# Attention values projected with tokens on partitions in one block, and keys kept in natural order

## The chip, the cores and the metric

The kernel runs on one core of a Trainium2 chip. The metric is device time in microseconds (us), the median of repeated runs. Engines are TensorE (PE in the rows, with PEld for its weight loads), VectorE (DVE), ScalarE (ACT), GpSimd (POOL) and SyncE (SP), which issues most of the DMAs.

## What is computed

One decoder layer: two token mixers run side by side on a normalised input, stick-breaking attention with 8 heads of 64 and a gated delta rule with 4 heads of 128, on 1024 tokens of 1024 channels. Both results are gated, projected, merged and projected once more. Cut to the part that the change touches:

```python
h    = rms_norm(x, pre_w)
proj = h @ w_in                         # all projections of both mixers, gates, merge gates
# stick-breaking attention, for each block of 128 queries and all keys up to it
z = einsum('bhqd,bhkd->bhqk', qb, kb) * scale
causal = k_pos < q_pos
log_keep = where(causal, -softplus(z), 0)
suffix = cumsum(log_keep, axis=3, reverse=True) - log_keep   # sum over the later keys
a = where(causal, exp(log_sigmoid(z) + suffix), 0)
o = einsum('bhqk,bhkd->bhqd', a, vb)
```

So a key's weight is sigmoid(z) times the product of sigmoid(-z) over all keys that lie between it and the query: a running product from the latest key back to the first.

## The kernel before

Every matrix product of a projection is made in three parts, since each operand is kept as a rounded value and its rest (`hi`, `lo`): hi·hi, hi·lo, lo·hi. `dense` (L224 and on, its product at L231) computes one half of a projection, 128 channels x 512 tokens, as 8 x 3 = 24 products of 128x512. Its weight slice is loaded by `load_w` (a DMA of 512 KB on SP's queue into one of two `raw` buffers, a cast on ScalarE, a subtraction on VectorE). A dense result lies in one of three PSUM buffers of pool `psd`. All other PSUM tiles, the scores `z`, the transposes `aT` and the results `av`, take turns in the five buffers of pool `psg`: a tile takes the buffer of the fifth one before it, and has to wait until that one has been read.

The normalised input `h` (`h_hi`, `h_lo`) lies with channels on partitions, so it serves as moving operand with the weights as stationary one, and the result has channels on partitions. Per pair of heads `p` (four pairs) the attention takes four projections: `sb_k` (keys, written in reversed token order, so that the latest key comes first), `sb_v` (values, channels on partitions, also reversed), `sb_g` (the branch gate; between its two halves the 8 transposes of `svT` that give `svn`, values with tokens on partitions) and `sb_q`. `fill(n)` is n projections of the merge gates (`mg`), 16 in all, that nothing in the attention needs; they are used as filler.

In the attention, `sb_z(p, g, a)` takes queries 256 g to 256 g + 255 of head `a` of the pair, in two blocks `qb`: score products into `z` pieces of at most 512 keys, two sigmoids of each on ScalarE (`kp`, what is kept; `bt`, what is taken), one scan on VectorE that turns `kp` into the running product (L812), one product on GpSimd that multiplies it into `bt` (L813). The names of the tiles carry these numbers: `z_2_0_7_1` is pair 2, head 0, block 7, second piece. `sb_av(p, g)` transposes `bt` tile by tile (`aT`, from tile c = 7 downward), copies each out of PSUM (odd c on VectorE, even c on ScalarE, the last two with the causal mask on VectorE) and multiplies it with `svn` into `av`. It runs one g behind: the transposes of g stand after the scores of g + 1.

The order on TensorE is what the generators write. `weave` takes steps of two generators in turn so that both progress in proportion to two given costs: here the attention of pair p, and a side chain that holds the projections of pair p + 1 and one filler (four fillers beside the last pair). Ahead of that stand the delta rule's scan, woven with `sb_k(0)` and `sb_v(0)`, then `sb_g(0)`, `sb_q(0)`, the delta rule's output and its branch projections `yb(0..7)`, and behind it the attention's branch projections (`ya`) and the output projection.

## Time and profile before

| | |
|---|---|
| median of three runs | 948.19 us (947.26 to 949.79) |
| profiled execution, its time | 947.04 us |
| its span, first to last instruction | 945.2 us |
| TensorE busy | 926.2 us, 98% of the span |
| VectorE / ScalarE / GpSimd busy | 588.6 / 384.4 / 167.0 us |
| 64 scans on VectorE | 101.9 us |
| 64 products on GpSimd behind them | 104.1 us |
| 32 transposes of `svT` on TensorE | four groups of 8, from 409.6 to 671.3 us |

The four pairs of the attention take about 475 to 548, 548 to 631, 631 to 714 and 714 to 803 us of the span, the branch projections `yb` 428 to 475, the output projection the last 95 us. Busy time of TensorE counts instructions that overlap their neighbour once; the pitch, from one start to the next, is what one costs. Idle time on an engine that nobody waits for costs nothing.

### The profile page before, as it was taken

What the parts mean: (1) busy time and instruction counts of PE and PEld (TensorE: products, weight loads), DVE (VectorE), ACT (ScalarE), POOL (GpSimd) and SP (SyncE); (2) the same over time, 40 slices, a digit from 0 to 9 for tenths busy, and PEclk for the clock granted to TensorE, in tenths of its full rate; (3) what the DMA queues carried; (4) which work ended last, traced back from release to release, by engine and by line L of the source; (5) the groups of instructions that cost most, each with busy time, mean ns of one, the idle gap of its engine ahead of it and who ended that gap; (6) DMA issues with size and microseconds to landing.
All of it is one profiled execution on the core that took longest, in us unless ns stands there. A gap on an engine that the chain in (4) does not pass through costs nothing.

```text
span 945.2 us, 13426 instructions
## 1 busy us (share of the span) xinstructions
PE 926.2 (98%) x5194; PEld 761.9 (81%) x5194; DVE 588.6 (62%) x1058; ACT 384.4 (41%) x853; POOL 167.0 (18%) x113
## 2 busy tenths in 40 slices
PE   8999999999999999999999999999999999999997
PEld 7968888788787887888888778877887887778886
DVE  5669895366999933656466634873684573953244
ACT  6666441145555112543254423543462453422121
POOL 1021210001113000000133212431332350441000
PEclk9999999999999999999999999999999999999999
DMA  8014214300232341015620111020101213841352
GB/s 261 10 46 123 79 67 134 68 24 23 68 78 76 109 104 37 23 45 204 219 68 23 45 45 45 23 68 23 45 23 45 90 45 125 303 160 36 102 182 96
DMA packets 84194, 80.12 MB, mean 85 GB/s; under 512 B 16969, under 2 KB 70306, under 8 KB 84130
## 3 DMA queue, kind: packets, MB, share of 16 engines
q1 hardware_dynamic: 80272, 70.55, 24.0%
q10 hardware_dynamic: 3858, 8.72, 2.7%
q8 instruction: 41, 0.67, 0.3%
q14 instruction: 23, 0.19, 0.1%
HBM read 60.88 MB, written 18.37 MB: 84 GB/s over the span
## 4 chain that ended last, share of the span: by engine, by line
PE 84%; DVE 9%; ACT 2%; issue 2%; DMA 1%; POOL 1%; DVEq 0%; POOLq 0%; ACTq 0%
PE d_mg L231 17%; PE y L1001 9%; PE d_sv L231 5%; PE d_sk L231 5%; PE d_gg L231 5%; PE d_sgt L231 5%; PE d_yb L231 4%; PE d_sq L231 4%; PE d_v L231 4%; PE av L842 3%; PE aT L829 3%; PE d_k L221 3%; PE d_k L231 2%; PE z L806 2%; PE z L807 2%
## 5 line engine op out<-in xcount | busy, mean ns | idle before, releaser
L813 POOL TENSOR_TENSOR bt<-bt,kp 128x127 f32<-128x127 f32 (+3 forms) x64 | 104.1, 1635 | 380.5 <-ACT bt L810 192.9
L812 DVE TENSOR_TENSOR_SCAN kp<-kp,mscan 128x128 f32<-128x128 f32 (+3 forms) x64 | 101.9, 1605 | 25.9 <-ACT kp L809 25.6
L231 PE MATMUL d_mg<-h_hi,whi_mg 128*128 128x512 f32 x256 | 101.5, 396 | 1.0 <-ACT mg L686 1.0
L231 PE MATMUL d_mg<-h_lo,whi_mg 128*128 128x512 f32 x256 | 99.9, 390 | 0.0
L231 PE MATMUL d_mg<-h_hi,wlo_mg 128*128 128x512 f32 x256 | 99.8, 390 | 0.0
L809 ACT ACTIVATE kp<-z 128x384 f32<-128x384 f32 (+4 forms) x96 | 48.2, 502 | 44.8 <-PE z L807 41.2
L231 PEld LDWEIGHTS d_mg<-h_hi,whi_mg 128*128 128x128 f32 x256 | 48.1, 188 | 12.5 <-issue 1.7
L231 PEld LDWEIGHTS d_mg<-h_hi,wlo_mg 128*128 128x128 f32 x256 | 48.1, 188 | 10.2
L231 PEld LDWEIGHTS d_mg<-h_lo,whi_mg 128*128 128x128 f32 x256 | 48.1, 188 | 9.2
L1001 PE MATMUL y<-wohi,m_lo 128*128 128x512 f32 (+1 forms) x136 | 51.3, 377 | 0.0
L1001 PE MATMUL y<-wohi,m_hi 128*128 128x512 f32 (+1 forms) x136 | 51.3, 377 | 0.0
L1001 PE MATMUL y<-wolo,m_hi 128*128 128x512 f32 (+1 forms) x136 | 51.2, 377 | 0.0
L810 ACT ACTIVATE bt<-z 128x384 f32<-128x384 f32 (+4 forms) x96 | 48.7, 508 | 3.7 <-DMA mB_d<-mb 1.7
L379 POOL TENSOR_TENSOR acc_k<-acc_k,pre_k 128x1024 f32<-128x1024 f32 x4 | 9.6, 2388 | 166.0 <-ACT pre_k L378 166.0
L842 PE MATMUL av<-aT,svn 128*64 128x256 f32 (+1 forms) x320 | 36.8, 366 | 1.1 <-DVE aT L835 1.1
L829 PE MATMUL aT<-ident,bt 128*128 128x128 f32 x288 | 36.6, 273 | 1.1 <-DVE sgT L849 0.6
L829 PEld LDWEIGHTS aT<-ident,bt 128*128 128x128 f32 x288 | 32.9, 140 | 5.7 <-issue 2.5
L89 DVE TENSOR_TENSOR wlo_mg<-raw_mg,whi_mg 128x1024 fp32r<-128x1024 f32 x16 | 24.3, 1517 | 20.3 <-ACT whi_mg L88 20.3
L1005 ACT ACTIVATE yj<-y 128x512 f32<-128x512 f32 (+1 forms) x17 | 9.7, 573 | 62.9 <-PE y L1001 56.6
L964 POOL TENSOR_TENSOR sA<-sA,mBl 128x512 f32<-128x512 f32 x16 | 25.5, 1606 | 48.7 <-DMA mBl<-mB_d 26.5
L842 PEld LDWEIGHTS av<-aT,svn 128*64 128x64 f32 x320 | 20.7, 136 | 15.8 <-issue 4.9
L686 ACT ACTIVATE mg<-d_mg 128x512 f32<-128x512 f32 x32 | 19.2, 602 | 30.9 <-PE d_mg L231 30.4
(379 smaller groups left out, 2450.3 us busy)
## 6 DMA issues: line engine op xcount, KB each, us to landing
raw_mg<-in_w_in_dram SPq DMA_DIRECT2D x16, 512.0 KB, 4.2
mg_d<-mg ACTq DMA_DIRECT2D x16, 512.0 KB, 2.9
x<-in_x_dram SPq DMA_DIRECT2D x8, 512.0 KB, 6.2
mb<-mg_d SPq DMA_DIRECT2D x8, 512.0 KB, 5.9
mB_d<-mb SPq DMA_DIRECT2D x8, 512.0 KB, 2.6
rawo<-in_w_out_dram SPq DMA_DIRECT2D x8, 512.0 KB, 4.4
sA<-mg_d SPq DMA_DIRECT2D x8, 512.0 KB, 7.1
mBl<-mB_d SPq DMA_DIRECT2D x8, 512.0 KB, 7.5
```

Source lines behind the costliest of these rows:

```text
L89: nc.vector.tensor_sub(lo[:, :nk], raw[:, :nk], hi[:, :nk].bitcast(F32))
L221: nc.tensor.matmul(ps, lhsT=a[:, k], rhs=b[:, c0:c1], start=(k == 0 and i == 0), stop=(k == nk - 1 and i == 2))
L231: nc.tensor.matmul(ps, lhsT=a[:, k], rhs=b[:, hs], start=(k == 0 and i == 0), stop=(k == nk - 1 and i == 2))
L686: nc.scalar.activation(gt[:, hs], ps, AF.Sigmoid)
L809: nc.scalar.activation(kp[:, os_], ps[:, :pc], AF.Sigmoid, scale=-0.125)
L810: nc.scalar.activation(bt[:, os_], ps[:, :pc], AF.Sigmoid, scale=0.125)
L812: nc.vector.tensor_tensor_scan(kp[:, :n], kp[:, :n], mscan[:, :n], 1.0, op0=ALU.mult, op1=ALU.max)
L813: nc.gpsimd.tensor_tensor(bt[:, 1:n], bt[:, 1:n], kp[:, 0:n - 1], op=ALU.mult)
L829: nc.tensor.transpose(ps[:, (a * 2 + j) * P:(a * 2 + j + 1) * P], at[p, a, qb][:, off:off + P], ident)
L842: nc.tensor.matmul(av[a * 64:(a + 1) * 64, j0 * P:2 * P], lhsT=vn[:, c, a * 64:(a + 1) * 64], rhs=aT[:, a * 2 + j0:a * 2 + 2], start=(c == ...
L964: nc.gpsimd.tensor_tensor(ga[:, hs], ga[:, hs], mb[:, hs], op=ALU.add)
L1001: nc.tensor.matmul(ps, lhsT=a[:, k, ts_], rhs=b[:, c0:c1], start=(k == 0 and i == 0), stop=(k == NK - 1 and i == 2))
```

## The change

Values are projected once, ahead of the attention, with the other operand stationary: a tile of 128 tokens of `h` is stationary and the weights of all 512 value channels move, so the result has tokens on partitions and needs no transpose. `load_wv` loads the weights in four pieces of 512 KB, after `yb(1)` to `yb(4)`, and splits them; `sb_v` then makes 8 token tiles of 24 products, each copied out by ScalarE. Keys and values stay in natural order. The scan runs over a reversed view of `kp`, the product on GpSimd reads the next column where it read the one before, the causal mask is mirrored, and the transposes take their columns from the other end.

The side chains of the attention lose the value projections, and the fillers are dealt out anew: one beside the delta rule in place of `sb_v(0)`, one after `sb_g(0)` in place of `sb_q(0)`, which moves behind the value block; one beside each of pairs 0 and 1, none beside pair 2, three beside pair 3. One is left for after the attention, as before.

```diff
-                                fill=0.0, base=-P, channel_multiplier=1)
+                                fill=0.0, base=-1, channel_multiplier=-1)
...
-            rs = slice((1 - half) * HT, (2 - half) * HT)
+            hs = slice(half * HT, (half + 1) * HT)
...
-                nc.scalar.copy(K[a][s, rs][:, ::-1], ps[s])
-                nc.vector.tensor_sub(K[a][d, rs][:, ::-1], ps[s], K[a][s, rs][:, ::-1].bitcast(F32))
+                nc.scalar.copy(K[a][s, hs], ps[s])
+                nc.vector.tensor_sub(K[a][d, hs], ps[s], K[a][s, hs].bitcast(F32))
...
-    def sb_v(p):
-        vT = slot(f"svT_{p}")
-        w = load_w(win[:, 1024 + p * P:1024 + (p + 1) * P], NK, f"sv{p}")
-        for half in range(2):
-            rs = slice((1 - half) * HT, (2 - half) * HT)
-            ps = yield from dense(w, NK, hk, half, f"sv{p}")
-            nc.scalar.copy(vT[:, rs][:, ::-1], ps)
-        sbd[p].append(vT)
+    wv, sv = [], []
+
+    def load_wv(k2):
+        with tc.high_priority(offset=ahead[0]):
+            raw = wp.tile([P, 2, HT], F32, tag="raw", name=f"raw_sv{k2}")
+            nc.sync.dma_start(raw, win[k2 * 2 * P:(k2 + 1) * 2 * P, 1024:1536].rearrange("(k p) c -> p k c", p=P))
+            hi = slot(f"svhi_{k2}", F32R, shape=[P, 2, HT])
+            lo = slot(f"svlo_{k2}", F32R, shape=[P, 2, HT])
+            nc.scalar.copy(hi, raw)
+            nc.vector.tensor_sub(lo, raw, hi.bitcast(F32))
+        for k in range(2):
+            wv.append((hi[:, k], lo[:, k]))
+
+    def sb_v():
+        for t in range(NT):
+            ts_ = slice(t * P, (t + 1) * P)
+            if t % 2 == 0:
+                sv.append(slot(f"sv_{t}", shape=[P, 2, HT]))
+            ps = psd.tile([P, HT], F32, tag="d", name=f"d_sv_{t}")
+            for k in range(NK):
+                rh, rl = hk(k)
+                for i, (a, b) in enumerate(((rh, wv[k][0]), (rh, wv[k][1]), (rl, wv[k][0]))):
+                    nc.tensor.matmul(ps, lhsT=a[:, ts_], rhs=b, start=(k == 0 and i == 0),
+                                     stop=(k == NK - 1 and i == 2))
+                yield 0.64
+            nc.scalar.copy(sv[t // 2][:, t % 2], ps)
...
-            if half == 0:
-                vT = sbd[p].pop()
-                vn = slot(f"svn_{p}", shape=[P, NT, P])
-                for g in range(2):
-                    ps = gps(f"svp_{p}_{g}")
-                    for j in range(4):
-                        c = g * 4 + j
-                        nc.tensor.transpose(ps[:, j * P:(j + 1) * P], vT[:, c * P:(c + 1) * P], ident)
-                    nc.vector.tensor_copy(vn[:, g * 4:g * 4 + 4], ps.rearrange("p (c j) -> p c j", j=P))
-                sbd[p].append(vn)
...
-    stages = (sb_k, sb_v, sb_g, sb_q)
+    stages = (sb_k, sb_g, sb_q)
...
-                nc.vector.tensor_tensor_scan(kp[:, :n], kp[:, :n], mscan[:, :n], 1.0, op0=ALU.mult, op1=ALU.max)
-                nc.gpsimd.tensor_tensor(bt[:, 1:n], bt[:, 1:n], kp[:, 0:n - 1], op=ALU.mult)
+                kr = kp[:, :n][:, ::-1]
+                nc.vector.tensor_tensor_scan(kr, kr, mscan[:, :n], 1.0, op0=ALU.mult, op1=ALU.max)
+                nc.gpsimd.tensor_tensor(bt[:, 0:n - 1], bt[:, 0:n - 1], kp[:, 1:n], op=ALU.mult)
...
-                    off = c * P - (T - (qb + 1) * P)
+                    off = (NT - 1 - c) * P
...
-    weave(sc, 37, chain(sb_k(0), sb_v(0)), 20.5)
+    weave(sc, 37, chain(sb_k(0), fill(1)), 20.5)
     g_n(1)
-    drain(sb_g(0), sb_q(0))
+    drain(sb_g(0), fill(1))
     g_o(2)
     g_o(3)
-    drain(*[yb(m) for m in range(NK)])
+    for m in range(NK):
+        drain(yb(m))
+        if 1 <= m <= 4:
+            load_wv(m - 1)
+    drain(sb_v(), sb_q(0))
...
-        side = chain(*[f(p + 1) for f in stages], fill(1)) if p + 1 < NP else fill(4)
-        weave(until_none(att), 24.0, side, 52.0 if p + 1 < NP else 41.0)
+        side = chain(*[f(p + 1) for f in stages], fill(p < 2)) if p + 1 < NP else fill(3)
+        weave(until_none(att), 24.0, side, (40.0 if p < 2 else 30.0))
```

Three places show how this moves instructions. The numbers at the ends of the names are buffer numbers.

TensorE, pair 2, between the transposes of tile 5 and of tile 4 of g = 1, before. All 27 dense products that stand there belong to the query projection of pair 3; the last three are shown.

```order
L231 MATMUL d_sq3_1_6280<-h_hi_189,whi_sq3_6241 128x512
L231 MATMUL d_sq3_1_6280<-h_lo_190,whi_sq3_6241 128x512
L231 MATMUL d_sq3_1_6280<-h_hi_189,wlo_sq3_6242 128x512
L829 MATMUL aT_2_1_4_6284<-ident_111,bt_2_0_3_6009 128x128
L829 MATMUL aT_2_1_4_6284<-ident_111,bt_2_1_3_6074 128x128
L806 MATMUL z_2_0_6_0_6290<-KA_2_5161,QH_2_1_5664 128x448
```

The same place after, all of it:

```order
L837 MATMUL aT_2_1_5_6293<-ident_111,bt_2_1_3_6167 128x128
L231 MATMUL d_sgt3_1_6238<-h_hi_189,whi_sgt3_6136 128x512
L231 MATMUL d_sgt3_1_6238<-h_lo_190,whi_sgt3_6136 128x512
L231 MATMUL d_sgt3_1_6238<-h_hi_189,wlo_sgt3_6137 128x512
L231 MATMUL d_sgt3_1_6238<-h_hi_189,whi_sgt3_6136 128x512
L231 MATMUL d_sgt3_1_6238<-h_lo_190,whi_sgt3_6136 128x512
L231 MATMUL d_sgt3_1_6238<-h_hi_189,wlo_sgt3_6137 128x512
L231 MATMUL d_sq3_0_6313<-h_hi_189,whi_sq3_6309 128x512
L231 MATMUL d_sq3_0_6313<-h_lo_190,whi_sq3_6309 128x512
L231 MATMUL d_sq3_0_6313<-h_hi_189,wlo_sq3_6310 128x512
L837 MATMUL aT_2_1_4_6317<-ident_111,bt_2_0_3_6110 128x128
L837 MATMUL aT_2_1_4_6317<-ident_111,bt_2_1_3_6167 128x128
```

Of the 27 dense products 9 are left; in pair 3 they go from 18 to 9. Between the transposes of tile 6 and of tile 5 of g = 2, ahead of `av`, they go from 18 to 9 in pairs 2 and 3, and stay 18 in pairs 0 and 1.

VectorE, pair 2, g = 2 and the two longest scans of head 1 (`kp_2_1_6`, `kp_2_1_7`), before:

```order
L89 TENSOR_TENSOR wlo_mg3_6542<-raw_mg3_6539,whi_mg3_6541 128x1024
L740 TENSOR_TENSOR QL_3_1_6354<-d_sq3_1_6280,QH_3_1_6353 64x512
L741 TENSOR_TENSOR QL_3_1_6354<-d_sq3_1_6280,QH_3_1_6353 64x512
L812 SCALAR_TENSOR_TENSOR kp_2_1_6_6343<-kp_2_1_6_6343,mscan_127 128x896
L835 COPY aT_2_2_7_6417<-aT_2_2_7_6418 128x512
L812 SCALAR_TENSOR_TENSOR kp_2_1_7_6402<-kp_2_1_7_6402,mscan_127 128x1024
L835 COPY aT_2_2_5_6450<-aT_2_2_5_6451 128x512
```

And after:

```order
L740 TENSOR_TENSOR QL_3_0_6387<-d_sq3_0_6313,QH_3_0_6386 64x512
L741 TENSOR_TENSOR QL_3_0_6387<-d_sq3_0_6313,QH_3_0_6386 64x512
L820 SCALAR_TENSOR_TENSOR kp_2_1_6_6367<-kp_2_1_6_6367,mscan_127 128x896
L740 TENSOR_TENSOR QL_3_0_6387<-d_sq3_0_6313,QH_3_0_6386 64x512
L741 TENSOR_TENSOR QL_3_0_6387<-d_sq3_0_6313,QH_3_0_6386 64x512
L843 COPY aT_2_2_7_6425<-aT_2_2_7_6426 128x512
L820 SCALAR_TENSOR_TENSOR kp_2_1_7_6410<-kp_2_1_7_6410,mscan_127 128x1024
L843 COPY aT_2_2_5_6447<-aT_2_2_5_6448 128x512
```

The query projection of pair 3 now stands later against the attention, and two of its subtractions have come between the two scans.

ScalarE at the start of the attention, after (before, the first sigmoids stood among the branch weights' casts, `whi_wbg4` and `whi_wbg6`, long after the casts of Q):

```order
L739 CAST QH_0_0_4735<-d_sq0_0_4710 64x512
L88 CAST whi_sgt1_4973<-raw_sgt1_4971 128x1024
L738 CAST QH_0_1_4770<-d_sq0_1_4745 64x512
L739 CAST QH_0_1_4770<-d_sq0_1_4745 64x512
L816 ACTIVATE kp_0_0_0_4780<-z_0_0_0_0_4782 128x128
L817 ACTIVATE bt_0_0_0_4781<-z_0_0_0_0_4782 128x128
```

The first sigmoids now stand behind a weight cast and two casts of the query projection's second half.

## Rows read from the trace of the kernel before

**Rows 1.** The page: busy time and share; the chain that ended last, by engine

```profile
PE 926.2 (98%) x5194; PEld 761.9 (81%) x5194; DVE 588.6 (62%) x1058; ACT 384.4 (41%) x853; POOL 167.0 (18%) x113
PE 84%; DVE 9%; ACT 2%; issue 2%; DMA 1%; POOL 1%; DVEq 0%; POOLq 0%; ACTq 0%
```

**Rows 2.** Two stretches: length, busy PE, PEld, DVE, ACT, POOL, granted clock, DMA

```profile
631.00:714.00 83.00, 82.69 (x453) 66.56 (x451) 50.33 (x55) 37.64 (x78) 26.62 (x16) 1.00 0.14 39
714.00:797.00 83.00, 82.69 (x454) 66.33 (x454) 43.84 (x41) 34.21 (x71) 26.61 (x16) 1.00 0.20 64
```

**Rows 3.** The chain in order of time: start, length, engine, what

```profile
416.09 10.88 PE d_sq L231 x48
...
856.23 80.12 PE y L1001 x366
```

**Rows 4.** Timeline of PE, start and length; line 781 (min/median/max ns)

```profile
512.70 1.03 PE L780 MATMUL svp<-ident,svT 128*128 128x128 f32 x8
513.49 0.48 PE L231 MATMUL d_sgt<-h_hi,whi_sgt 128*128 128x512 f32 x1
...
L781 DVE COPY svn<-svp x8: 683/688/692, 410.2 to 672.4; 128x512 f32<-128x512 f32 x8
```

**Rows 5.** Lines 753 and 740 on DVE: min/median/max ns

```profile
L753 DVE TENSOR_TENSOR KA<-d_sk,KA x8: 683/685/685, 373.0 to 652.0; 64x512 fp32r<-64x512 f32 x8
L753 DVE TENSOR_TENSOR KB<-d_sk,KB x8: 692/694/694, 374.4 to 653.3; 64x512 fp32r<-64x512 f32 x8
...
L740 DVE TENSOR_TENSOR QL<-d_sq,QH x16: 674/690/696, 422.8 to 702.6; 64x512 fp32r<-64x512 f32 x16
```

**Rows 6.** Timelines of PE and of DVE, pair 3, g = 1

```profile
754.86 0.30 PE L806 MATMUL z<-KB,QH 128*128 128x320 f32 x1
...
762.78 0.40 PE L806 MATMUL z<-KA,QH 128*128 128x512 f32 x1
...
761.43 0.99 DVE L833 TENSOR_TENSOR aT<-aT,mdiag 128x512 f32<-128x512 f32 x2
```

**Rows 7.** Timelines of PE and of DVE, pair 3, g = 2

```profile
781.65 1.95 PE L842 MATMUL av<-aT,svn 128*64 128x256 f32 x16
...
781.33 0.66 DVE L835 COPY aT<-aT 128x512 f32<-128x512 f32 x1
```

**Rows 8.** Timelines of PE, DVE and POOL, pair 2, g = 2

```profile
710.05 2.14 PE L842 MATMUL av<-aT,svn 128*64 128x256 f32 x16
...
693.39 2.98 DVE L812 TENSOR_TENSOR_SCAN kp<-kp,mscan 128x1024 f32<-128x1024 f32 x1
...
706.66 3.81 DVE L812 TENSOR_TENSOR_SCAN kp<-kp,mscan 128x1024 f32<-128x1024 f32 x1
710.39 0.66 DVE L835 COPY aT<-aT 128x512 f32<-128x512 f32 x1
...
692.10 2.12 POOL L813 TENSOR_TENSOR bt<-bt,kp 128x895 f32<-128x895 f32 x1 [4.38 <-DVE kp L812]
...
706.19 2.12 POOL L813 TENSOR_TENSOR bt<-bt,kp 128x895 f32<-128x895 f32 x1 [7.25 <-ACT aT L837]
```

**Rows 9.** Timelines of PE and ACT; line 738 (min/median/max ns)

```profile
432.38 0.22 PE L806 MATMUL z<-KA,QH 128*128 128x128 f32 x1
...
548.00 1.05 ACT L88 CAST whi_sv<-raw_sv 128x1024 fp32r<-128x1024 f32 x1 [4.66 <-PE d_mg L231]
...
549.44 0.27 ACT L809 ACTIVATE kp<-z 128x128 f32<-128x128 f32 x1
...
L738 ACT CAST QH<-d_sq x16: 579/582/585, 421.6 to 701.3; 64x512 fp32r<-64x512 f32 x16
```

**Rows 10.** Waits of PE: total us, times, longest

```profile
PE av L842 <- DVE aT L835: 1.1, 1, 1.1
```

**Rows 11.** The page's scans (busy, mean ns); DMA issues, us to landing

```profile
L812 DVE TENSOR_TENSOR_SCAN kp<-kp,mscan 128x128 f32<-128x128 f32 (+3 forms) x64 | 101.9, 1605 | 25.9 <-ACT kp L809 25.6
...
raw_sv<-in_w_in_dram SPq DMA_DIRECT2D x4, 512.0 KB, 4.2
```

More of the change, by code (lines that the diff above doesn't have):

```diff
@@ L772, in sb_g @@
             nc.vector.tensor_tensor(gT[:, hs], gT[:, hs], ps, op=ALU.mult)
-            if half == 0:
-                vT = sbd[p].pop()
-                vn = slot(f"svn_{p}", shape=[P, NT, P])
-                for g in range(2):
-                    ps = gps(f"svp_{p}_{g}")
-                    for j in range(4):
-                        c = g * 4 + j
-                        nc.tensor.transpose(ps[:, j * P:(j + 1) * P], vT[:, c * P:(c + 1) * P], ident)
-                    nc.vector.tensor_copy(vn[:, g * 4:g * 4 + 4], ps.rearrange("p (c j) -> p c j", j=P))
-                sbd[p].append(vn)
         sbd[p].append(gT)
         osb.append(gT)
-    stages = (sb_k, sb_v, sb_g, sb_q)
+    stages = (sb_k, sb_g, sb_q)
     at = {}
     def sb_z(p, g, a):
-        K, vn, gT, Q = sbd[p]
+        K, gT, Q = sbd[p]
         QH, QL = Q[g // 2]
@@ L796, in sb_z @@
                 n = (qb + 1) * P
-                c0 = T - n
                 qs = slice((qb % 4) * P, (qb % 4 + 1) * P)
@@ L803, in sb_z @@
                 for i in range(npc):
-                    cs = slice(c0 + i * pc, c0 + (i + 1) * pc)
+                    cs = slice(i * pc, (i + 1) * pc)
                     ps = gps(f"z_{p}_{a}_{qb}_{i}")
@@ L811, in sb_z @@
                     yield 2 * pc / 2400 + 0.06 * (i == 0)
-                nc.vector.tensor_tensor_scan(kp[:, :n], kp[:, :n], mscan[:, :n], 1.0, op0=ALU.mult, op1=ALU.max)
-                nc.gpsimd.tensor_tensor(bt[:, 1:n], bt[:, 1:n], kp[:, 0:n - 1], op=ALU.mult)
+                kr = kp[:, :n][:, ::-1]
+                nc.vector.tensor_tensor_scan(kr, kr, mscan[:, :n], 1.0, op0=ALU.mult, op1=ALU.max)
+                nc.gpsimd.tensor_tensor(bt[:, 0:n - 1], bt[:, 0:n - 1], kp[:, 1:n], op=ALU.mult)
                 at[p, a, qb] = bt
     def sb_av(p, g):
-        K, vn, gT, Q = sbd[p]
+        K, gT, Q = sbd[p]
         gq = slice(g * 2 * P, (g + 1) * 2 * P)
@@ L840, in mm @@
         def mm(c, j0, aT):
+            kb = NT - 1 - c
             for a in range(2):
-                nc.tensor.matmul(av[a * 64:(a + 1) * 64, j0 * P:2 * P], lhsT=vn[:, c, a * 64:(a + 1) * 64],
+                ds = slice(p * P + a * 64, p * P + (a + 1) * 64)
+                nc.tensor.matmul(av[a * 64:(a + 1) * 64, j0 * P:2 * P], lhsT=sv[kb // 2][:, kb % 2, ds],
                                  rhs=aT[:, a * 2 + j0:a * 2 + 2], start=(c == NT - 1), stop=(c == cl))
```

## The prediction, made before the changed kernel was run

> **What bounds the kernel now.** I read the page's busy shares first: TensorE is busy 98% of the span, VectorE 62%, ScalarE 41%, GpSimd 18%, and the chain that ended last is 84% TensorE [rows 1]. The table by stretches says the same where the change acts: in a stretch of 83 us of the attention TensorE is busy 82.7 us, VectorE 50.3 and then 43.8 [rows 2]. So an instruction removed from TensorE is worth its pitch, one removed from VectorE or ScalarE nothing by itself, and a wait that opens on TensorE costs its whole length. The dense projections are what fills TensorE between the attention's own steps; their pitch is 10.88/48 = 227 ns [rows 3]. TensorE's granted clock is 1.00 in the attention, the upper of its two levels (2.4 GHz), and the change leaves no long pause on TensorE, so I keep it there.
>
> **What is removed.** Four times, 8 transposes of v stand between two dense products. They start at 512.70, the next dense product at 513.49 [rows 4]: 0.79 us for 8, that is 99 ns each, and up to 0.1 us for the switch back. 4 x 0.79 = 3.2 us, 4 x 0.88 = 3.5 us with the slower products after each switch; I take **-3.5 us**, bounds -3.2 and -3.9. The 8 copies that drained them, 0.688 us each [rows 4], leave VectorE, 5.5 us in all, off the path.
>
> **What costs nothing.** v itself takes 192 dense products before (8 halves of 24) and 192 after (8 token tiles of 24). Stationary and moving operand change places, but the output product at the end already runs with activations stationary and weights moving: 80.12 us for 366 instructions, 219 ns [rows 3], so the pitch stays. Each half, or token tile, is copied out by ScalarE once either way; the new loads are four of 512 KB, as the removed ones were, with the same split. Reversed views: K's low half is now written forward instead of backward; the backward form takes 685 or 694 ns, the forward one of the same size for Q 690 ns [rows 5]. No row shows a scan over a reversed view. The bound from below is nothing gained; from above, double the scan's time (a rival below). I take zero, as the nearest row is a reversed read and write on the same engine that costs nothing.
>
> **What is moved.** The merge-gate blocks are the filler. Before, five projections of two halves each (48 products, 10.88 us) run beside each of the first three head pairs of the attention and four beside the last; now four, four, three and three. Five blocks, 54.4 us, are thereby taken out of the attention: v as one block ahead, the first query projection after it, and two gates earlier still. Their own time is not lost, but where the attention waits for VectorE, there is less under which to wait. Four places by the order, priced by the trace:
>
> 1. *Third and fourth pair, queries 256 to 511 (g=1).* The order has 27 products between the transposes of tile 5 and of tile 4 before in pair 2, 18 in pair 3, now 9 in both. The score tile that closes this stretch (z_7, second piece) takes the PSUM buffer of aT_5, five allocations back, and so waits until VectorE has masked it. In pair 3 today the mask starts at 761.43 and takes about 0.68 us, ended 762.1; the score starts at 762.78 [rows 6], 0.7 us late enough. With 9 products fewer (9 x 227 ns = 2.04 us) it is ready at 760.74 and waits 1.4 us. VectorE's chain there (scan of 640, copy, scan of 768, mask) starts from the score at 754.86, which stands before those 9, so it doesn't come earlier. Pair 2 has the same chain and the same 9 products: **+1.4 us twice**, bounds 0.5 and 2.0.
>
> 2. *Pair 3, the two longest scans.* Today 18 products stand between the transposes of tiles 7, 6 and of 5; then av runs and needs the copy of tile 5, which VectorE makes after the scan of 1024: the copy ends at 781.33 + 0.66 = 781.99. av starts at 781.65 and reaches tile 5 after 4 products of 105 ns (16 in 1.95 us, the last one's 0.37 counted once), at 782.07 [rows 7]. There is no slack. With 9 products fewer it arrives at 780.03: **+2.0 us**, bounds 1.0 and 2.5.
>
> 3. *Pair 2, the same place.* av reaches tile 5 at 710.05 + 0.42 = 710.47, the copy ends at 710.39 + 0.66 = 711.05 [rows 8]: 0.6 us of wait today. Now 9 products stand there, not 18, and two of the query projection's subtractions (0.69 each, [rows 5]) stand in VectorE's queue between the scan of 896 and the copy of tile 7, which the scan of 1024 is queued behind. Does their 1.37 us come on top? The scan of 1024 began at 706.66 and took 3.81, while GpSimd's product ran from 706.19 to 708.31: 1.65 us under it and 2.16 after. Elsewhere it took 2.98 (693.39 to 696.37), with GpSimd's product ending at 692.10 + 2.12 = 694.22: 2.15 after [rows 8]. So the scan needs 2.15 us from the end of GpSimd's product, and the subtractions lie beside that product: the scan ends 708.31 + 2.15 = 710.46, as today. av waits 711.1 - 708.4 = 2.7 us in place of 0.6: **+2.1 us**, bounds 1.0 and 3.5, the upper where the subtractions count in full (+1.4).
>
> The Trainium skill says this of the mechanism ("SBUF — State Buffer", section "SBUF: two separate sides"): VectorE and GpSimd share a port pair that is locked for a whole instruction, by a VectorE operation with two SBUF inputs against a GpSimd one that reads SBUF, and the loser waits in full. The two durations agree with it; by that rule place 3 costs 2.1 us and the total is 4.6, without it 3.5 and 6.0.
>
> 4. *Start of the attention.* Before, the first score tiles were issued inside the branch projections (z at 432.38, [rows 9]). Now they follow the first query projection at once. The sixth of them needs the PSUM buffer of the first, which ScalarE frees after two casts of Q (0.58 each, [rows 9]) and two sigmoids of 128 columns (0.27 each, [rows 9]) behind a weight cast of 1.05 us. From the end of the query projection: 0.3 (a guess at the hand-over) + 1.16 + 0.54 = 2.0 us, with the weight cast 3.05; TensorE has 5 score tiles (1.0 us) and 4 products (0.9 us) there. The wait is 0.1 to 1.2 us, then about 0.5 each at the seventh tile and the first transpose: **+1.2 us**, bounds 0 and 3.
>
> In pair 0 the order keeps 18 products at the place of step 2, and today's wait of 1.1 us for that copy [rows 10] stays; in pair 1 it keeps 18 as well. Both: 0, bounds -1.1 and +1. The Q subtractions that leave the start of the branch projections are worth at most 0.3 us.
>
> **Sum.** -3.5 + 2 x 1.4 + 2.0 + 2.1 + 1.2 = **+4.6 us**. On the profiled execution (947.04, span 945.2) that is 951.6; on the median of the three runs, 948.19, it is 952.8, since the profiled run lay 1.15 below it. I state 952.2, between the two.
>
> **Rivals.**
> - *Cover still suffices (faster).* The waits of steps 1 to 3 exist only if VectorE's chain starts where I put it. It has lost 1.4 us of copies in each of the first three pairs and at least one weight split in all four; if it gets to each scan 2 us earlier, the 9 products that went are not missed. For it: VectorE is busy only 43.8 of 83 us in pair 3. Against: each chain starts with a score tile, not with VectorE's backlog. Time: 947.0 - 3.5 + 1.2 = 944.7, or 943.5 without step 4.
> - *About half of the waits.* A wait at step 1 lets VectorE run ahead, and step 3's subtractions may land before the scan: -3.5 + 1.2 + 3.7 = +1.4, 948.4 to 949.6. It reads as no change.
> - *The loads of v (slower).* Four loads of 512 KB now stand in SP's queue among those of the branch weights and gates, and use the same raw buffers; a wait on a free buffer holds every load behind it. If a branch weight comes one landing late (4.2 us for 512 KB, [rows 11]), TensorE waits for it, once or twice: 952.2 + 4.2 = 956.4. It decides from the point where a branch weight is issued later than 5.4 us, one branch projection of 24 products, before its first use.
> - *A reversed scan is slower.* The 64 scans take 101.9 us [rows 11]; if twice that, VectorE has 50.3 + 25 = 75 us in a pair whose TensorE work is now about 70: some 5 us in each of three pairs and more waits, 970. Against it: the reversed rows above.
> - *The change doesn't do what it says*: the order shows that the transposes and copies are gone, so there is no such case.
>
> The Trainium skill ("Vector Engine (DVE) Microarchitecture Reference", section 5.1) lists how the engine streams an operand with a negative step as not measured; the reversed subtraction above is the only row here, and the rival's small chance is from it.
>
> **Chances.** Forecast 0.47; cover suffices 0.22; half of the waits 0.18; loads 0.09; reversed scan 0.04. About 0.3% (2.8 us) is what a measurement of this kernel can tell from no change: 945.4 to 951.0 reads as the same. The forecast's own spread (bounds of steps 1 to 4: 948 to 956) puts about a fifth of its chance into "same". So: faster 0.22, same 0.28, slower 0.50. The range goes from 943.5 (all cover) to 957.0 (one late load), and leaves out about 0.15.
>
> **What would show it.** Right: after the change TensorE waits of 1 to 1.5 us at the score tile z_7 and 2 to 3 us at av, released by VectorE's aT mask or copy, in the last two pairs and not in the first two; dense pitch 227 ns in the v block; scans of 896 near 2.02 us. Wrong: no TensorE wait over 0.5 us in the last two pairs (first rival), waits on the split of branch weights between 428 and 475 us (third), or a scan of 896 well above 2.02 us (fourth).

## The result, and the profile after

The changed kernel takes 955.85 us (median of 4 runs, 954.87 to 956.34), the kernel before on the same chips 948.8 (947.26 to 949.79). The ratio is 1.0074, with a 95% interval of 1.0057 to 1.0092: 7 us slower. The profiled execution took 956.34, its span is 954.6; the span of before was 945.2, so the two traces differ by 9.4 us, some 2 us more than the medians.

The page of the changed kernel, busy time and share [rows 1], then the scans [rows 11] and GpSimd's products:

```profile
PE 927.8 (97%) x5162; PEld 759.6 (80%) x5162; DVE 578.6 (61%) x1050; ACT 384.1 (40%) x853; POOL 157.3 (16%) x113
...
L821 POOL TENSOR_TENSOR bt<-bt,kp 128x127 f32<-128x127 f32 (+3 forms) x64 | 94.4, 1485 | 395.7 <-DVE kp L820 350.0
L820 DVE TENSOR_TENSOR_SCAN kp<-kp,mscan 128x128 f32<-128x128 f32 (+3 forms) x64 | 98.1, 1555 | 23.1 <-ACT kp L816 22.5
```

VectorE and GpSimd each work 10 us less than before, and the kernel is slower: neither was the bound. Where the time went is read from three stretches between the same marks, the first branch projection `yb`, the first `ya` product and the first output product. The columns are those of [rows 2]. Before:

```profile
428.40:803.10 374.70, 372.41 (x1980) 300.48 (x1978) 220.43 (x235) 157.41 (x315) 104.11 (x64) 1.00 0.22 71
803.10:850.80 47.70, 45.17 (x195) 35.70 (x194) 34.84 (x38) 15.80 (x21) 22.35 (x14) 1.00 0.63 233
850.80:945.20 94.40, 87.91 (x409) 73.10 (x407) 36.92 (x91) 19.53 (x50) 3.18 (x3) 0.98 0.30 104
```

After:

```profile
428.80:811.10 382.30, 372.84 (x1956) 298.50 (x1954) 215.82 (x233) 159.17 (x317) 94.35 (x64) 1.00 0.22 69
811.10:860.20 49.10, 45.72 (x194) 35.57 (x193) 33.34 (x38) 15.64 (x21) 22.26 (x14) 1.00 0.61 226
860.20:954.60 94.40, 87.89 (x409) 73.14 (x407) 36.91 (x91) 19.52 (x50) 3.22 (x3) 0.99 0.29 103
```

7.6 us are lost between `yb` and `ya`, where the change is; 1.4 us in the branch projections of the attention that follow, which the change does not touch; 0.4 us ahead of both, and the output projection is alike to 0.1 us. As means of whole stretches the granted clocks are alike too, 1.00, 1.00 and 0.98 or 0.99; the mean hides one place in the attention, shown in the next section.

The waits of TensorE in the first stretch after (line waited, line waited for, total us, times, longest):

```profile
PE av L852 <- DVE aT L843: 4.9, 3, 2.5
PE z L813 <- DVE aT L841: 2.1, 3, 1.3
PE aT L837 <- DVE aT L843: 0.7, 2, 0.5
PE aT L837 <- ACT bt L817: 0.5, 2, 0.3
PE aT L837 <- POOL bt L821: 0.5, 1, 0.5
PE z L813 <- ACT bt L817: 0.4, 1, 0.4
PE aT L837 <- DVE sgT L859: 0.3, 1, 0.3
```

Together 9.4 us, where the kernel before has 2.2 (the 1.1 of [rows 10], and 0.6 and 0.5 at transposes). The view lists idle time only, from the end of one product to the start of the next, and a product is listed as longer than the pitch: a score product starts at 553.92 and the next, which waits, at 555.61, 1.69 later; at a pitch of 0.23 that is 1.46 lost, listed as 1.29. Counted by pitch (start to start, less what the same step usually takes), the gaps over 0.2 us cost 11.6 us after and 3.1 before.

### The profile page after: what moved, and what is told of

Read it like the earlier page. It is cut to its first block, busy times and chain, and to the rows that moved or that the text cites. A ratio compares the mean times of both kernels' runs of the same rounds, so it can differ in the third digit from the quotient of the medians.

```text
span 954.6 us, 13336 instructions
## 1 busy us (share of the span) xinstructions
PE 927.8 (97%) x5162; PEld 759.6 (80%) x5162; DVE 578.6 (61%) x1050; ACT 384.1 (40%) x853; POOL 157.3 (16%) x113
## 5 line engine op out<-in xcount | busy, mean ns | idle before, releaser
L821 POOL TENSOR_TENSOR bt<-bt,kp 128x127 f32<-128x127 f32 (+3 forms) x64 | 94.4, 1485 | 395.7 <-DVE kp L820 350.0
L820 DVE TENSOR_TENSOR_SCAN kp<-kp,mscan 128x128 f32<-128x128 f32 (+3 forms) x64 | 98.1, 1555 | 23.1 <-ACT kp L816 22.5
L740 DVE TENSOR_TENSOR QL<-d_sq,QH 64x512 fp32r<-64x512 f32 x16 | 11.0, 688 | 60.4 <-ACT QH L739 57.7
L852 PE MATMUL av<-aT,sv 128*64 128x256 f32 (+1 forms) x320 | 37.1, 367 | 4.9 <-DVE aT L843 4.9
L852 PEld LDWEIGHTS av<-aT,sv 128*64 128x64 f32 x320 | 20.7, 136 | 19.6 <-DVE aT L843 6.4
```

The source lines that it names most:

```text
L740: nc.vector.tensor_sub(QL[s, a], ps[s], QH[s, a].bitcast(F32))
L820: nc.vector.tensor_tensor_scan(kr, kr, mscan[:, :n], 1.0, op0=ALU.mult, op1=ALU.max)
L821: nc.gpsimd.tensor_tensor(bt[:, 0:n - 1], bt[:, 0:n - 1], kp[:, 1:n], op=ALU.mult)
L852: nc.tensor.matmul(av[a * 64:(a + 1) * 64, j0 * P:2 * P], lhsT=sv[kb // 2][:, kb % 2, ds], rhs=aT[:, a * 2 + j0:a * 2 + 2], start=(c == NT ...
```

## The longest wait: pair 1

The longest wait, 2.49 us, and one of 0.47 us just ahead of it are at one place, g = 2 of pair 1. Timelines of the changed kernel, TensorE, ScalarE, VectorE (start, length, engine, what):

```profile
649.77 0.36 PE L813 MATMUL z<-KB,QH 128*128 128x448 f32 x1
...
658.06 0.44 PE L837 MATMUL aT<-ident,bt 128*128 128x128 f32 x2 [0.47 <-DVE aT L843]
658.43 1.08 PE L852 MATMUL av<-aT,sv 128*64 128x256 f32 x8
662.01 1.30 PE L852 MATMUL av<-aT,sv 128*64 128x256 f32 x8 [2.49 <-DVE aT L843]
...
649.57 0.55 ACT L817 ACTIVATE bt<-z 128x448 f32<-128x448 f32 x1 [2.39 <-POOL bt L821]
650.01 0.57 ACT L738 CAST QH<-d_sq 64x512 fp32r<-64x512 f32 x1
650.59 0.58 ACT L739 CAST QH<-d_sq 64x512 fp32r<-64x512 f32 x1
652.62 0.58 ACT L738 CAST QH<-d_sq 64x512 fp32r<-64x512 f32 x1 [1.45 <-DVE QL L741]
653.21 0.58 ACT L739 CAST QH<-d_sq 64x512 fp32r<-64x512 f32 x1
653.82 0.55 ACT L816 ACTIVATE kp<-z 128x448 f32<-128x448 f32 x1
...
651.21 0.68 DVE L740 TENSOR_TENSOR QL<-d_sq,QH 64x512 fp32r<-64x512 f32 x1 [0.25 <-ACT QH L739]
655.26 2.02 DVE L820 TENSOR_TENSOR_SCAN kp<-kp,mscan 128x896 f32<-128x896 f32 x1
657.93 3.44 DVE L820 TENSOR_TENSOR_SCAN kp<-kp,mscan 128x1024 f32<-128x1024 f32 x1
661.29 0.66 DVE L843 COPY aT<-aT 128x512 f32<-128x512 f32 x1
```

Read it from the end. `av` waits until 662.01 for the copy of tile 5, which stands behind the scan of 1024, which stands behind the scan of 896. That scan starts at 655.26, although its score was made at 649.77: the score's sigmoid runs at 653.82 only, since ScalarE has four casts of the next query projection ahead of it in its queue. They start at 650.01 only, behind a sigmoid that has waited 2.39 us for a product of GpSimd, and the third of them waits 1.45 us for VectorE's subtractions, the first of which has itself waited for the second cast. In the order of the kernel before 27 products stand between the two pieces of that score, after the change 18: 2 us less in which the casts could be done. The count that the prediction looked at, behind the score, stayed at 18.

The cost of this wait doesn't end with it. Right behind it the granted clock of TensorE falls to 0.50, the lower of its two levels (1.2 of 2.4 GHz), and comes back to 1.00; the columns are those of [rows 2]:

```profile
662.80:666.10 3.30, 3.30 (x11) 2.28 (x8) 1.02 (x2) 0.00 (x0) 0.74 (x1) 0.50 0.00 0
666.20:669.30 3.10, 3.10 (x22) 2.40 (x22) 0.82 (x1) 1.71 (x3) 0.00 (x0) 1.00 0.00 0
```

Seven dense products take from 663.24 to 666.28, 3.04 us where 7 x 0.227 is 1.59: about 1.5 us lost, in products that start late without a wait in any list. The trace before has no such place in the attention. Three traces of the experiments have it, each time behind or in a wait at `av`. A wait of 1.45 us in pair 2 of the changed kernel has none behind it, and one as long in an experiment has, so the length of the wait alone doesn't decide it; what does is not shown.

## The experiments

All are compared with the kernel before on their own chip, 947.9 to 948.1 us.

**Keys in natural order alone.** The kernel before with the reversed view, the shifted product and the mirrored mask, values still transposed:

```diff
-                nc.gpsimd.tensor_tensor(bt[:, 1:n], bt[:, 1:n], kp[:, 0:n - 1], op=ALU.mult)
+                kr = kp[:, :n][:, ::-1]
+                nc.vector.tensor_tensor_scan(kr, kr, mscan[:, :n], 1.0, op0=ALU.mult, op1=ALU.max)
+                nc.gpsimd.tensor_tensor(bt[:, 0:n - 1], bt[:, 0:n - 1], kp[:, 1:n], op=ALU.mult)
...
-                    off = c * P - (T - (qb + 1) * P)
+                    off = (NT - 1 - c) * P
```

> The kernel before with the second half of the change alone: keys in natural order, reversed view for the scan, GpSimd's product one column to the other side, mirrored mask. Values are still projected per pair and transposed, all fillers stay. Theory (the loss comes from the missing cover): no loss here; GpSimd's product gets shorter as in the changed kernel (128x895 in 1.77 us against 2.12, 128x1023 in 2.00 against 2.38), scans of 896 stay at 2.02, and the time is that of the kernel before or up to 2 us less (946 to 949). Rival (the reversed scan is the cause): 3 us or more slower, with scans of 896 above 2.02 us.

Measured: 946.43 us, ratio 0.9987 (0.9977 to 0.9997). The key order costs nothing and is worth about 1 us. The rival with the slow reversed scan is out.

**The transposes left out.** The kernel before without the 32 transposes and 8 copies:

> The kernel before with the 32 transposes of the values and their 8 copies left out (av uses the values untransposed); everything else stands. Theory: TensorE is the bound, so the time falls by 32 x 99 to 110 ns, 3.2 to 3.9 us: about 945.2. Rival (something else stands ready behind the transposes): it falls by less than 1.5 us.

Measured: 945.04 us, ratio 0.9976 (0.9964 to 0.9988): 2.3 us, between 1.1 and 3.4; the stretch from `yb` to `ya` of its trace is 371.9 us, 2.8 less than before. The gain is there, and smaller than the 3.5 us of the sum.

**Four gates ahead of the attention.** To the first experiment's kernel, one edit, without anything of the value block:

```diff
+    drain(fill(4))
     att = attention()
...
-        side = chain(*[f(p + 1) for f in stages], fill(1)) if p + 1 < NP else fill(4)
-        weave(until_none(att), 24.0, side, 52.0 if p + 1 < NP else 41.0)
+        side = chain(*[f(p + 1) for f in stages]) if p + 1 < NP else fill(3)
+        weave(until_none(att), 24.0, side, 40.0 if p + 1 < NP else 30.0)
```

> e1 (kernel before with keys in natural order, 946.4) with one edit: four of the seven gate projections that stand beside the attention are put ahead of it, so that 4, 4, 4 and 3 projections are left beside the pairs. No value block, no new loads of v, transposes as before. Theory (the loss is the missing cover): 4 to 7 us slower than e1, 950.5 to 953.5, with TensorE waits at av and at the score z_7 released by VectorE's copies and masks. Rival (the loss comes with the value block, its loads or its slots): within 1.5 us of e1.

Measured: 951.14 us, 4.7 more than 946.43; ratio to the kernel before 1.0034 (1.0022 to 1.0046). The waits of TensorE between `yb` and `ya`, where the first experiment's kernel has 1.8 us:

```profile
PE av L842 <- DVE aT L835: 1.7, 3, 1.0
PE av L842 <- ACT aT L837: 0.9, 2, 0.4
PE z L805 <- DVE aT L833: 0.4, 1, 0.4
```

With 0.2 us at a transpose that is 3.2 us. The same products in another place cost about 5 us, without the value block, its loads or its slots. The two traces differ by 6.5 us; 2.9 of them lie between `yb` and `ya` (376.7 us against 373.8) and 2.0 in `ya` (49.4 against 47.4), the two stretches in which the changed kernel loses as well. Another 1.6 lie ahead of both, where this trace has the lower clock once (0.50 from 260.8 to 264.0) and that of the first experiment doesn't.

**Cover given back.** Two kernels add the five missing projections to the changed kernel, as work that nobody needs (54.5 us of products). In the first they stand at the end of the side chains:

```diff
-        side = chain(*[f(p + 1) for f in stages], fill(p < 2)) if p + 1 < NP else fill(3)
-        weave(until_none(att), 24.0, side, (40.0 if p < 2 else 30.0))
+        side = chain(*[f(p + 1) for f in stages], fill(p < 2), dummy(2 if p == 2 else 1, p)) if p + 1 < NP else chain(fill(3), dummy(1, p))
+        weave(until_none(att), 24.0, side, 52.0 if p + 1 < NP else 41.0)
```

> The changed kernel with five projections more in the attention that nobody needs (they compute gates again): one beside pairs 0, 1 and 3, two beside pair 2, so that each pair has as much dense work beside it as in the kernel before, and the costs of weave are those of before. The work added is 240 products of 227 ns, 54.5 us, to 955.9: 1010.4 if nothing else changes. Theory (the waits come from missing cover): the 9 to 10 us of waits in the attention go back to those 3.7 of before, 8 to 9 us less, so about 1001 to 1003. Rival (the waits come with the new order of queues, whatever the cover): 1008 to 1011.

Measured: 1005.92 us. 955.85 + 54.5 = 1010.4, so 4.4 us came back, neither 8 nor none. In the second one each stands where the kernel before had a value projection, behind the keys:

```diff
+        side = (chain(sb_k(p + 1), dummy(1, p), sb_g(p + 1), sb_q(p + 1), fill(1) if p < 2 else dummy(1, 3)) if p + 1 < NP
+                else chain(fill(3), dummy(1, p + 1)))
```

> As e3 (the changed kernel with five unneeded projections beside the attention, 54.5 us of products), but each stands where the kernel before had its work: the stand-in for a pair's value projection directly behind the keys, the gate at the end. Amount of cover as in e3, order of the side chain as in the kernel before. e3 took 1005.9, so it got back 4.4 of about 9 us. Theory in its second form (waits come from missing cover and from where the query projection's casts fall): the rest comes back as well, 1000.5 to 1003. Rival (the amount alone counts, and e3 shows all that it gives): 1005 to 1007.

Measured: 1000.98 us: 9.4 us came back, as much as the change had lost (7.05) and the transposes' gain (2.3) together. Amount and order count about alike, 4.4 and 5.0 us. The two are not wholly apart: the first of these kernels moves the casts too, and its trace has the lower clock behind its longest wait (0.50 from 585.1 to 588.4), some 1.5 us, where that of the second has none. The waits of TensorE at `av` in the first kernel and in the second:

```profile
PE av L852 <- DVE aT L843: 4.5, 3, 2.3
```

```profile
PE av L852 <- DVE aT L843: 2.2, 2, 1.5
```

**The query projection moved.** Two kernels change only the order of the side chain in the changed kernel. Query ahead of the gate:

```diff
-    stages = (sb_k, sb_g, sb_q)
+    stages = (sb_k, sb_q, sb_g)
```

> The changed kernel with the query projection ahead of the gate projection in each side chain (keys, queries, gate), nothing else. In pair 1 of the changed kernel the second piece of the score z_6 waits 4 us in ScalarE's queue behind casts of the query projection, which wait for VectorE, and av then waits 2.8 us. Theory: with the query casts out of that stretch, the waits at av in pair 1 (2.8 and 0.6 us) go, and in pair 2 up to 1 us: 952 to 953. Rival (only the number of dense products counts): 955 to 957, the waits stay where they are.

Measured: 955.88 us, no change. The wait in pair 1 is gone, as expected, but the casts fall into other scores: its trace has 1.2 us at `av` in pair 0, 2.2 us in pair 2, and 1.8 us at transposes that wait for ScalarE. Its two largest waits between `yb` and `ya`:

```profile
PE av L852 <- DVE aT L843: 4.3, 3, 2.2
PE aT L837 <- ACT bt L817: 1.8, 4, 1.0
```

Query last, with the filler of pairs 0 and 1 behind the keys:

```diff
-        side = chain(*[f(p + 1) for f in stages], fill(p < 2)) if p + 1 < NP else fill(3)
+        side = (chain(sb_k(p + 1), fill(p < 2), sb_g(p + 1), sb_q(p + 1)) if p + 1 < NP else fill(3))
```

> The changed kernel with only the order of the side chain of pairs 0 and 1 changed: keys, gate projection of the merge, branch gate, queries (the query projection last). The amount of cover is that of the changed kernel. e4 moved the query projection forward and the waits moved with it; here it moves backward. Theory: pair 1's waits (2.8 and 0.6 us) shrink to those of pair 2, which has that order (1.7 and 0.9 us), and pair 0 gets new ones of about as much: 954.5 to 956.5. Rival (the order alone was at fault, as e5 against e3 lets think): 951 to 953.

Measured: 952.06 us, ratio 1.0040 (1.0027 to 1.0053): 3.8 us less than the changed kernel. My theory said that the waits would only move; the rival was right. They fell: `av` waits 3.1 us in all (2.7 for VectorE, 0.4 for ScalarE), where it waited 4.9, and in pair 1 0.75 of 2.5. Its trace, of the slowest of six runs, has the lower clock behind the wait of 1.45 us in pair 2 (0.50 from 724.2 to 727.5).

**The first query projection back where it was**, which leaves one gate more for pair 2:

```diff
-    drain(sb_g(0), fill(1))
+    drain(sb_g(0), sb_q(0))
...
-    drain(sb_v(), sb_q(0))
+    drain(sb_v())
```

> The changed kernel with the first query projection back where the kernel before has it (behind the gate of pair 0), so that one more gate projection is left for the attention; it goes beside pair 2: 4, 4, 4, 3. The start of the attention no longer stands behind casts of Q. Theory: the waits at the start (0.6 us and the slow seventh tile, about 1 us) go, and the third pair's 3.6 us of waits fall by 1 to 2.5 us: 952.5 to 954. Rival (what pair 2 lacks is not cover): 955 to 956.

Measured: 961.42 us, ratio 1.0142 (1.0126 to 1.0157), and neither theory had that. The wait at the start went, but `av` in pair 2 waits 4.8 us and a branch projection 1.5, and the 2.5 us of pair 1 stay. Both waits at `av` have the lower clock behind them (0.50 from 651.5 to 654.8 and from 729.9 to 733.3). All four runs of this kernel show a mean granted clock of 0.990 to 0.992, where those of all others compared here show 0.995 or more, so the clock has a part in the 5.6 us over the changed kernel. VectorE's copy of tile 5 there:

```profile
723.51 3.45 DVE L820 TENSOR_TENSOR_SCAN kp<-kp,mscan 128x1024 f32<-128x1024 f32 x1
729.16 0.69 DVE L843 COPY aT<-aT 128x512 f32<-128x512 f32 x1 [2.20 <-POOL bt L821]
```

The copy waits 2.2 us for GpSimd's product. The query tiles now hold four of the 25 slots through the branch projections, and all later tiles fall into other slots; that the copy's target slot is one that GpSimd still reads is how I understand this row, and it was not tested.

**Values in two halves.** A version meant to keep the gain and the cover: 256 channels ahead of the attention, the other 256 beside pair 1, four or five projections beside each pair:

```diff
-    drain(sb_v(), sb_q(0))
+    drain(sb_v(0))
...
+        side = (sb_k(1), sb_g(1), sb_q(1), fill(1)), (sb_k(2), sb_v(1, True), sb_g(2), sb_q(2)), (sb_k(3), fill(1), sb_g(3), sb_q(3)), (fill(4),)
+        weave(until_none(att), 24.0, chain(*side[p]), (42.0, 52.0, 42.0, 41.0)[p])
```

> A version meant to keep both: values with tokens on partitions, but in two halves of 256 channels, the first ahead of the attention, the second beside pair 1; the first query projection stays where the kernel before has it; fillers so that 4, 5, 4 and 4 projections stand beside the pairs. A product of 128x256 is not in any trace with a 128-wide stationary operand; if it takes half of 227 ns the work is the same. Theory: 3 us of transposes gained, half to all of the new waits gone: 945 to 950. Rival (a 256-wide product costs more than half, as its weight load of 140 to 190 ns is not hidden): 8 to 14 us of extra product time, 955 or more.

Measured: 946.29 us, ratio 0.9979 (0.9970 to 0.9989), 9.6 us less than the changed kernel. TensorE waits 1.6 us between `yb` and `ya`. The narrower product costs a little more than half. Its timeline, two neighbours:

```profile
473.68 0.28 PE L782 MATMUL d_sv<-svhi,h_hi 128*128 128x256 f32 x1
473.80 0.28 PE L782 MATMUL d_sv<-svlo,h_hi 128*128 128x256 f32 x1
```

A pitch of 0.120 us against 0.227 for 512 columns: 384 x 0.120 = 46.1 us for all values, where 192 x 0.227 = 43.6 would do; most of the transposes' gain goes there. With the filler of pair 0 behind the keys as well:

> e9 (values in two halves, 946.3) with one edit: the filler beside pair 0 stands behind the keys, where the kernel before had the value projection, and not at the end of the side chain, so that the order of all side chains is that of the kernel before. Theory (order of the side chain and amount of cover set the waits): pair 0 has only 0.6 us of wait left in e9, so at most that goes: 945.5 to 946.5. Rival (moving the query projection backward costs waits, as in e6): 947 to 949.

Measured: 945.54 us, ratio 0.9979 (0.9970 to 0.9988). It can't be told from the version before it. Both beat the kernel before by 0.2% and the changed kernel by 1%; both are no faster than the key order alone by more than the intervals allow.

**The first gate loads ahead of the output weights**, on the version in two halves, because of the 1.4 us in `ya`:

```diff
+    first_g = slot("sA_0"), slot("mBl_0")
+    nc.sync.dma_start(first_g[0], mg_d[0])
+    nc.sync.dma_start(first_g[1], mB_d[0])
     rawo = [load_wo(0, k2) for k2 in range(4)]
```

> e9 (values in two halves, 946.3) with the first loads of the merge gates (sA_0, mBl_0) issued ahead of the four loads of the output weights. In e9 VectorE's first use of sA_0 waits 1.2 us for its load, in the changed kernel about 2.4 us. Theory (that wait makes the branch projections longer): 1 to 2 us less than e9, 944.5 to 945.5, and the stretch from the first branch product to the first output product falls from 48.0 to about 47. Rival (the stretch is bound by VectorE and ScalarE anyway): within 0.5 us of e9.

Measured: 952.37 us, 6 us slower, and the stretch from `ya` to the output products grew from 48.0 to 52.4. Another 1.6 us of the two traces lie ahead of the attention, where this one has the lower clock once (0.50 from 260.6 to 263.8). The wait for the load is gone, and another took its place: VectorE's wait for ScalarE's `m_hi`, here and, in the second fence, in the version without the edit.

```profile
DVE m_lo L972 <- ACT m_hi L971: 17.3, 9, 2.1
```

```profile
DVE m_lo L969 <- ACT m_hi L968: 9.4, 5, 2.2
```

VectorE's queue there is `sA`, `m_lo`, `sA`, `m_lo`; each `m_lo` needs the cast of a sum that GpSimd makes of the `sA` before it. Once VectorE has caught up, this ring runs at 3.4 us a half (three of them from its timeline), and TensorE's 12 products take 2.7:

```profile
837.59 0.68 DVE L987 TENSOR_TENSOR sA<-sA,d_ya 128x512 f32<-128x512 f32 x1
840.99 0.68 DVE L987 TENSOR_TENSOR sA<-sA,d_ya 128x512 f32<-128x512 f32 x1
844.32 0.68 DVE L987 TENSOR_TENSOR sA<-sA,d_ya 128x512 f32<-128x512 f32 x1
```

So the stretch should get longer with the number of halves that run in this ring, which was not tested by itself. TensorE waits for `sA` 4 times before the change, 6 times after it and 7 times here. What puts the changed kernel there rather than the kernel before was not tried.

**A tail for two prices** behind the last store of the kernel before:

> The kernel before with a tail behind its last store: GpSimd products of 128x1023 with output and second input each starting at column 0 or 1 (four forms, three of each), then VectorE scans of 128x1024 forward and over a reversed view in turn, with GpSimd idle. Open from the traces: why GpSimd's product is shorter after the change. If it is the column where the output starts, forms with output at column 0 take 2.0 and forms at column 1 take 2.4 us; if it is the second input's column, the other split; if neither, all alike. The scans: forward and reversed both 2.15 to 2.3 us if the view costs nothing.

The four forms of GpSimd's product (output and first input, second input: columns 1, 0; 0, 1; 0, 0; 1, 1), then scans forward and reversed:

```profile
952.20 2.34 POOL L1027 TENSOR_TENSOR mt<-mt,mt 128x1023 f32<-128x1023 f32 x1
954.62 2.00 POOL L1028 TENSOR_TENSOR mt<-mt,mt 128x1023 f32<-128x1023 f32 x1
956.69 2.34 POOL L1029 TENSOR_TENSOR mt<-mt,mt 128x1023 f32<-128x1023 f32 x1
959.11 2.34 POOL L1030 TENSOR_TENSOR mt<-mt,mt 128x1023 f32<-128x1023 f32 x1
...
976.18 2.29 DVE L1033 TENSOR_TENSOR_SCAN mt<-mt,mscan 128x1024 f32<-128x1024 f32 x1
978.50 2.29 DVE L1035 TENSOR_TENSOR_SCAN mt<-mt,mscan 128x1024 f32<-128x1024 f32 x1
```

A reversed scan takes what a forward one takes. GpSimd's product is shorter in one form only, output at column 0 and second input at column 1, which is the changed kernel's; none of the three guesses was right.

## Why the prediction was right, and where its steps and sizes were off

The direction and the mechanism held: dense work taken out of the attention opens waits on TensorE that cost more than the transposes were worth. 952.2 was forecast, +4.6 on the sum; 955.85 was measured, +7.05, inside the range of 943.5 to 957.0 and near its upper end. Its own sign was met by half: the last two pairs have waits at `z_7` (0.57 and 0.28 us) and at `av` (1.45 and 0.94), smaller than stated, but the first two pairs, which should have had none, have 1.3 and 2.5. Step by step:

- **Transposes, -3.5.** Measured 2.3 (1.1 to 3.4), by the trace 2.8. Too large by about 1 us. Nothing waited in their place: TensorE's waits at `av` stayed at 1.0 us.
- **What costs nothing.** Right for the scan (2.02 us for 896 columns before and after, 2.29 in the tail) and for the value block: its 192 products take from 472.68 to 516.20, 227 ns each. The shorter GpSimd product was missed; it may be what the first experiment's 1 us comes from.
- **Step 1, the score z_7 in pairs 2 and 3, 1.4 us each.** The mechanism is there, smaller: 0.57 and 0.28 us idle. GpSimd's product of 640 columns is shorter, so the scan of 768 behind it starts its work sooner (2.59 us against 2.85 at the same place in pair 3). Missed: pair 0 has the same wait, 1.3 us. In pair 0 the order took 9 products at this place too (27 to 18), and VectorE has key subtractions and a weight split of 2.59 us in its queue there. The step counted products in pairs 2 and 3 and did not look at pair 0. The wait of 1.1 us at `av` in pair 0 that was to stay is gone there, and this one stands in its place.
- **Step 2, pair 3 at av, 2.0 us.** 0.94 idle, 1.1 by pitch: the mechanism as forecast, the size too large, for two reasons. In the traces each product of `av` is two records (the page counts 320 for 160 products; 16 are in the 1.95 us of [rows 7]), and the sum took the 105 ns of a record for a product. Eight records and not four stand ahead of tile 5 (x8 at 658.43 above), so `av` came to it half a microsecond later than put (782.57 and not 782.07), and where the prediction says that there is no slack there was that much. And the scan of 1024 ahead of the copy took 3.94 before and takes 3.59 now, since GpSimd's product beside it takes 1.78 in place of 2.12.
- **Step 3, pair 2 at av, 2.7 us in place of 0.6.** 1.45 at av, 0.25 and 0.32 ahead of it at the transposes, 2.0 together, 2.5 by pitch. The 0.6 us that it gave the kernel before are the same miscount: by pitch `av` lost 0.14 there (16 records in 2.14 us in [rows 8], in 1.95 in [rows 7]). The question whether the two subtractions come on top is answered nearly as forecast. VectorE and GpSimd there, after:

```profile
722.65 0.69 DVE L740 TENSOR_TENSOR QL<-d_sq,QH 64x512 fp32r<-64x512 f32 x1
723.36 0.69 DVE L741 TENSOR_TENSOR QL<-d_sq,QH 64x512 fp32r<-64x512 f32 x1
724.09 0.69 DVE L843 COPY aT<-aT 128x512 f32<-128x512 f32 x1
724.81 2.29 DVE L820 TENSOR_TENSOR_SCAN kp<-kp,mscan 128x1024 f32<-128x1024 f32 x1
...
722.85 1.77 POOL L821 TENSOR_TENSOR bt<-bt,kp 128x895 f32<-128x895 f32 x1 [2.95 <-DVE kp L820]
```

  GpSimd's product ends at 724.62, under the subtractions and the copy, and the scan behind takes 2.29, its time alone, where it took 3.81 in [rows 8]. It ends 2.48 us after GpSimd's product, 2.15 there: of the 1.37 us of subtractions 0.3 came on top. The Trainium skill's rule of the exclusive port ("SBUF — State Buffer", "SBUF: two separate sides") agrees with that.
- **Step 4, the start, 1.2 us.** 0.43 idle at the sixth score, 0.6 by pitch: in the range, and half as large.
- **Pair 1, 0 us.** This is the step that failed. It asked how many products stand between a score and the copy that av needs (18, as before), and not how many stand ahead of that score, nor what ScalarE has in its queue there. The wait was 2.5 and 0.5 us, the largest of all. With the order changed so that the query casts do not fall ahead of that score, it went in one experiment and shrank to 0.75 us in another.
- **The clock, kept at 1.00.** This failed with it. The prediction kept the upper level because the change leaves no long pause on TensorE; the wait in pair 1 was one, and about 1.5 us went at 0.50 behind it.
- **`ya`, not in the sum.** 1.4 us came from a stretch that the change does not touch.

By pitch, the waits between `yb` and `ya` grew by 8.5 us (11.6 less 3.1) where the sum had 8.1. That the two are so near is luck: pairs 2 and 3 got 4.8 us where the sum had 6.9, and the rest came in pairs 0 and 1, where it had 1.2 at the start alone. With 1.5 for the clock and 2.8 for the transposes that makes 7.2 of the 7.6 us; 0.4 us stay unassigned.

The first rival (cover still suffices) is ruled out by the waits, and by the experiment that moves four gates alone. The second (about half of the waits) has the time against it; in pairs 2 and 3 two thirds came, but not by its mechanism, since the subtractions stood between the two scans. The late loads of v did not happen: TensorE has no wait of 0.2 us or more in the branch projections after the change. The reversed scan is ruled out twice.

## What to carry to other kernels

Independent work beside a chain of dependent steps is cover, and its worth is not its own time but the waits that it hides: before moving it away, count the products at each place where the bound engine would wait, ahead of the chain's first step as well as behind it, in every repetition. A projection beside such a chain also brings casts and subtractions into the other engines' queues; where they fall moved this kernel by 4 to 5 us at the same amount of work. A saving of 3 us that needs such a move should be tried in a form that leaves the cover in place: here two halves beat the one block by 9.6 us, though they can't be told from the kernel that has the key order alone.

## What was not expected of the hardware

GpSimd's product of two 128x1023 tiles takes 2.00 us with output at column 0 and second input at column 1, and 2.34 in the other three forms; the trace of the attention shows the same pair for 895 columns, 1.77 and 2.12. Which addresses decide it stays open. A product of 128x256 with a stationary operand of 128x128 has a pitch of 0.120 us, 6% more than half of the 0.227 for 512 columns. And a wait of TensorE can cost more than its length: in the changed kernel the clock stood at 0.50 from 662.8 to 666.1, right behind the longest wait, for about 1.5 us more.
